# Hyena filter beside the first wave: tap loads up to two quarters ahead, and the Abs tied to the shifted input

## The chip, the cores and the metric

The kernel runs on one core of one Trainium2 chip. The metric is the time of one execution in device microseconds; the kernel before has a median of 2582.66 us in three runs (2580.7 to 2584.5).

## What is computed

One layer of a hybrid backbone: a half-step SwiGLU on the latent tokens `x` and the context tokens `ctx` (256 each, width 2048), token mixing by grouped-query attention and a Hyena long convolution side by side, an output projection, and a second half-step SwiGLU on `x`. Each part is normed and modulated with shift, scale and gate from `w_ada`. Cut to what matters here, with the Hyena filter:

```python
def half_ffn(s, m, slot, g, w_up, w_down):
    h = modulate(rms_norm(s, g), chunk(m, 3 * slot), chunk(m, 3 * slot + 1))
    return s + 0.5 * chunk(m, 3 * slot + 2) * swiglu(h, w_up, w_down)

def hyena_filters(L, w1, b1, w2, b2, w3, b3, w4, freq, decay):
    ...                                    # positional features z, t in 0..1
    h = jnp.sin(fr * (z @ w1 + b1))
    h = jnp.sin(fr * (h @ w2 + b2))
    h = jnp.sin(fr * (h @ w3 + b3))
    h = (h @ w4).reshape(L, 2, HYENA_WIDTH)            # forward and backward half
    h = h * jnp.exp(-t[:, :, None] * jnp.abs(decay)[None])
    ...
    return kk / jnp.sum(jnp.abs(kk), axis=0, keepdims=True)

def reference(x, c, ctx, c_ctx, w_ada, ...):
    mod = silu(c) @ w_ada + b_ada          # 9 chunks of 2048: shift, scale, gate of three parts
    x = half_ffn(x, mod, 0, ...); ctx = half_ffn(ctx, mod_c, 0, ...)
    ...                                    # attention with rotary, Hyena with hyena_filters, output projection
    return half_ffn(x, mod, 2, ...)
```

The filter depends on no token: it is computed from weights alone, `HYENA_WIDTH` = 1024 channels times two halves, and its spectrum is needed only in the token mixing, far behind the first SwiGLU.

## The kernel before

Products are made in fp32 by splitting each operand into a rounded part and a remainder (`hi`, `lo`) and multiplying three times, so each weight tile costs a cast on ScalarE (`whi`) and a subtraction on VectorE (`wlo`).

**The first wave** is the beginning of the first SwiGLU. Nothing of `x` can be multiplied before its shift and scale are known, so the wave runs over the 16 chunks `d` of 128 model columns, and makes three output tiles (`WAVE` = 3) at once, as chunk after chunk of the modulated input comes up. One iteration `d` of the loop at L990 has in its source:

- `row_on(d + 1)`: 32 narrow matmuls (L197) of the conditioning vectors with two row loads `wrow` of 1 MB each, for the modulation of chunk d + 1; then `row_load` of the next row (L184, on SP's queue, four buffers);
- the tile of output 0 (`f1.tile`, L254 to L256), one step of the filter (`next(steps)`), then `col_on(d + 1)`: ScalarE copies the row (L204), TensorE turns it (L206), VectorE finishes shift and scale (L209 to L212), and `wave_h(d + 1)` makes the shifted input: L919 on VectorE, the pair L921 on ScalarE (`f1.shifted` is the second one), L923 on VectorE;
- the tile of output 1, a step; the tile of output 2, a step.

In every fourth iteration three weight tiles of 512 KB are loaded on POOL's queue (L1005, shown at L231), behind a gate, a tiny POOL copy (L1003) of the shift of chunk d, in iterations 1, 5 and 9; the casts and remainders of the tiles in use (L243, L247) are made in iterations 3, 7 and 11.

**The filter** (`filter_spectrum`) is a generator that is stepped between the tiles. After three sine layers (L692 to L714, up to iteration 3) come four quarters `q` of 256 channels, in three iterations each. In source order the Abs of quarter q lies at the beginning of iteration 3q + 4. A quarter does: Abs of the decay row on ScalarE, in place (L725); two Exps (L729) into new tiles; the split of the last layer's weights (L731, L732); the last layer's matmuls (L736, L737), sums and differences (L743, L744), absolute values and their sum (L748 to L754), the transform (L765), and the store of the spectrum to DRAM (`spec`, L773, on POOL's queue). `load_taps(q)` loads the decay rows and the last layer's weights of a quarter: two DMAs each (L684, L687), 128 KB apiece, on POOL's queue, into two tiles of the common pool `U` of 58 tiles of 2 KB a partition. Before, the taps of quarter q + 1 are loaded at the beginning of quarter q (L722), the slot at the end of iteration 3q + 3.

**The order of work.** Dependences, semaphores and buffers are set by a scheduler that orders the instructions of each engine when the program is built. An engine's queue is then worked off strictly in that order. The scheduler may put an instruction ahead of its place in the source when it takes its inputs to be ready. `then(a, do, ...)` (L274) gives it an edge: what `do` issues may not be placed ahead of `a` on the same engine. In the wave nearly all matmuls are chained in this way (`mm = then(mm, ...)`); the filter's steps are not.

## Time and profile before

| | |
|---|---|
| median of three runs | 2582.66 us (2580.7 to 2584.5) |
| the profiled execution | 2580.55 us |
| its span, first to last instruction | 2578.8 us |
| mean granted TensorE clock | 0.997 |
| TensorE busy | 2557.4 us (99%) |
| VectorE / ScalarE / POOL busy | 2164.0 / 1213.6 / 364.0 us |
| HBM read | 558.73 MB |

The profile tells of one execution. Times are microseconds from the first instruction. PE is TensorE's matmuls, PEld its weight loads, DVE VectorE, ACT ScalarE, POOL GpSimd, SP SyncE; a "q" behind the name is the engine's sequencer. `pb<-ident,sg` is what an instruction writes and reads, by the program's tile names. A row of the order of time gives start, duration, engine, line, operation, tiles, shapes, count of merged instructions, and in brackets the idle time of the engine ahead of it and what ended that. A row of the waits gives the waiting instruction, what it waited for, the sum, the count and the longest one. The time of a DMA is that from its issue to its landing. The wave takes about the first 155 us.

### The profile page before, as it was taken

The page shows a single profiled execution, that of the slowest core. Times are in us where ns is not written, and L with a number is a line of the kernel's source. Part 1 is how long each engine was busy: PE and PEld are TensorE (multiplying, and loading weights), DVE is VectorE, ACT ScalarE, POOL GpSimd, SP SyncE. Part 2 cuts the span into 40 slices and gives each one's busy share as a digit, 9 for nine tenths or more (in the row PEclk, how much of TensorE's full clock was granted, in tenths as well). Part 3 has the DMA queues.
Part 4 walks back from the last instruction along what each step waited for, and adds up shares of the span by engine and source line. Part 5 has one row for each costly group of instructions (what it writes and reads, how often), then busy time and mean ns, then how long its engine had stood idle before and what let it go on. Part 6 is the DMA issues. An engine that isn't in the chain of part 4 may idle for free.

```text
span 2578.8 us, 38723 instructions
## 1 busy us (share of the span) xinstructions
PE 2557.4 (99%) x14333; PEld 2199.4 (85%) x14333; DVE 2164.0 (84%) x3498; ACT 1213.6 (47%) x1702; POOL 364.0 (14%) x587
## 2 busy tenths in 40 slices
PE   8999999999999999999999999999999999999999
PEld 5678999999999999888888988888878888888887
DVE  6776888888888886777989796789789899999998
ACT  5353444444444443111211455457466666665554
POOL 1122222222222223320011000000000001012010
PEclk9999999999999999999999999999999999999999
DMA  9988889898888889996798555435757778789784
GB/s 364 355 288 221 233 247 259 240 259 245 244 240 253 250 256 305 395 377 203 258 331 290 185 164 188 131 117 162 233 168 235 247 240 264 238 266 309 236 285 159
DMA packets 209388, 640.77 MB, mean 248 GB/s; under 512 B 24716, under 2 KB 27757, under 8 KB 204845
## 3 DMA queue, kind: packets, MB, share of 16 engines
q1 hardware_dynamic: 134396, 482.37, 55.4%
q0 software_dynamic: 74608, 155.78, 23.3%
q8 instruction: 112, 1.84, 0.3%
q14 instruction: 80, 0.65, 0.1%
q10 hardware_dynamic: 192, 0.13, 0.0%
HBM read 558.73 MB, written 48.53 MB: 235 GB/s over the span
## 4 chain that ended last, share of the span: by engine, by line
PE 96%; DMA 2%; DVE 1%; ACT 0%; issue 0%; POOL 0%; SPq 0%; DVEq 0%; ACTq 0%; POOLq 0%
PE pb L254 10%; PE pb L255 9%; PE pb L256 9%; PE pa L254 9%; PE pa L255 9%; PE pa L256 9%; PE pa L1393 6%; PE pa L1394 6%; PE pa L1395 6%; PE pb L1393 4%; PE pb L1394 4%; PE pb L1395 4%; PE pa L262 3%; PE pa L264 2%; PE pa L1109 1%; PE pa L1110 1%
## 5 line engine op out<-in xcount | busy, mean ns | idle before, releaser
L243 ACT CAST whi<-raw 128x1024 fp32r<-128x1024 f32 x235 | 247.1, 1052 | 499.7 <-PE pb L255 187.8
L247 DVE TENSOR_TENSOR wlo<-raw,whi 128x1024 fp32r<-128x1024 f32 x235 | 286.8, 1221 | 133.7 <-ACT whi L243 131.1
L254 PE MATMUL pa<-u,whi 128*128 128x256 f32 (+1 forms) x912 | 307.4, 338 | 2.1 <-ACT u L906 2.1
L255 PE MATMUL pa<-u,whi 128*128 128x256 f32 (+1 forms) x912 | 305.3, 335 | 0.4 <-DVE u L911 0.4
L256 PE MATMUL pa<-u,wlo 128*128 128x256 f32 (+1 forms) x912 | 305.1, 335 | 0.0
L254 PE MATMUL pb<-u,whi 128*128 128x256 f32 (+1 forms) x904 | 300.2, 332 | 0.0
L255 PE MATMUL pb<-u,whi 128*128 128x256 f32 (+1 forms) x904 | 298.5, 330 | 0.0
L256 PE MATMUL pb<-u,wlo 128*128 128x256 f32 (+1 forms) x904 | 298.4, 330 | 0.0
L466 ACT CAST bhi<-raw 128x768 fp32r<-128x768 f32 x111 | 92.5, 833 | 265.7 <-PE pb L255 132.5
L158 DVE CUSTOM_DVE_ANT_0 adas<-adaw,crow,cond 128x1024 bf16<-128x1024 f32 x160 | 204.9, 1281 | 13.6 <-DMA adaw<-in_w_adaT_dram 11.8
L158 DVE CUSTOM_DVE_ANT_0 adas<-adaw,crow,mod 128x1024 bf16<-128x1024 f32 x160 | 204.9, 1281 | 13.2 <-DMA adaw<-in_w_adaT_dram 11.2
L254 PEld LDWEIGHTS pa<-u,whi 128*128 128x128 f32 x912 | 173.3, 190 | 24.7 <-issue 4.9
L255 PEld LDWEIGHTS pa<-u,whi 128*128 128x128 f32 x912 | 173.6, 190 | 17.5 <-DVE u L911 1.5
L256 PEld LDWEIGHTS pa<-u,wlo 128*128 128x128 f32 x912 | 173.8, 191 | 17.1
L254 PEld LDWEIGHTS pb<-u,whi 128*128 128x128 f32 x904 | 171.8, 190 | 17.4 <-issue 2.0
L469 DVE TENSOR_TENSOR blo<-raw,bhi 128x768 fp32r<-128x768 f32 x111 | 106.2, 957 | 94.6 <-ACT bhi L466 94.6
L255 PEld LDWEIGHTS pb<-u,whi 128*128 128x128 f32 x904 | 171.9, 190 | 15.8 <-issue 0.4
L256 PEld LDWEIGHTS pb<-u,wlo 128*128 128x128 f32 x904 | 171.8, 190 | 15.6
L1395 PE MATMUL pa<-whi,u 128*128 128x512 f32 x451 | 175.7, 390 | 0.0
L1393 PE MATMUL pa<-whi,u 128*128 128x512 f32 x450 | 175.7, 391 | 0.0
L1394 PE MATMUL pa<-wlo,u 128*128 128x512 f32 x450 | 175.6, 390 | 0.0
L277 ACT CAST whi<-raw 128x1024 fp32r<-128x1024 f32 x122 | 126.9, 1052 | 98.2 <-DVE raw L277 62.9
(477 smaller groups left out, 6687.8 us busy)
## 6 DMA issues: line engine op xcount, KB each, us to landing
adaw<-in_w_adaT_dram SPq DMA_DIRECT2D x224, 512.0 KB, 5.9
raw<-in_w_up1q_dram SPq DMA_DIRECT2D x124, 512.0 KB, 5.3
raw<-in_w_up2p_dram SPq DMA_DIRECT2D x107, 512.0 KB, 4.7
raw<-in_w_dn_dram SPq DMA_DIRECT2D x94, 512.0 KB, 5.9
u<-act POOLq DMA_DIRECT2D x172, 256.0 KB, 9.6
wrow<-in_w_ada_dram SPq DMA_DIRECT2D x32, 1024.0 KB, 9.6
raw<-in_w_dn2p_dram SPq DMA_DIRECT2D x59, 512.0 KB, 5.2
vraw<-in_w_up2p_dram SPq DMA_DIRECT2D x53, 512.0 KB, 4.8
```

Of the source, the lines that this page charges most:

```text
L158: V.tensor_tensor_reduce(out=sc, in0=t, in1=crow[i][:, b * (D // 2) : (b + 1) * (D // 2)], scale=1.0, scalar=mcol if b else bada[:, c * KT ...
L243: last_hi[0] = S.copy(hi, raw)
L247: last_lo[0] = V.tensor_sub(lo, raw, hi.bitcast(F32))
L254: PE.matmul(ps, w[0], xx[0], start=start, stop=False)
L255: PE.matmul(ps, w[0], xx[1], start=False, stop=False)
L256: return PE.matmul(ps, w[1], xx[0], start=False, stop=stop)
L277: return do(*args, **kw)
L466: return raw, hi, lo, S.copy(hi, raw[:, :, 0:3])
L469: return V.tensor_sub(lo, raw[:, :, 0:3], hi.bitcast(F32))
L1393: PE.matmul(ps[t], hi, w[0], start=start, stop=False)
L1394: PE.matmul(ps[t], hi, w[1], start=False, stop=False)
L1395: last = PE.matmul(ps[t], lo, w[0], start=False, stop=stop)
```

## The change

Taps are held in a list that is now read from its front. Quarter 0's are loaded in the second sine layer as before; quarter 1's right behind the load of the DFT matrix (`mats`) in the third layer; quarter 2's and 3's in the third step of quarters 0 and 1, behind the sums and differences. The Abs is issued with an edge to `f1.shifted`, the latest shifted input at that point of the source.

```diff
                 mats = U((P, 2, 2, P))
                 nc.gpsimd.dma_start(mats, a["fdft"])
+                taps.append(load_taps(1))
...
         for q in range(4):
-            now = taps.pop()
-            if q < 3:
-                taps.append(load_taps(q + 1))
+            now = taps.pop(0)
             dec, w4 = now
             yield
-            S.activation(dec, dec, AF.Abs)
+            then(f1.shifted, S.activation, dec, dec, AF.Abs)
...
                 V.tensor_sub(pm_[:, 1, :], kt[:, 0, :], kt[:, 1, :])
                 pm.append(pm_)
+            if q < 2:
+                taps.append(load_taps(q + 2))
             yield
```

## The prediction

> **What bounds the kernel now.** I read the page first, then who waited for whom on TensorE, then the order of time around the one long wait, then short stretches.

> ```profile
> span 2578.8 us, 38723 instructions
> ...
> PE 2557.4 (99%) x14333; PEld 2199.4 (85%) x14333; DVE 2164.0 (84%) x3498; ACT 1213.6 (47%) x1702; POOL 364.0 (14%) x587
> ```

> TensorE sets the end. It is idle for 2578.8 - 2557.4 = 21.4 us in all, so a change that leaves the matmuls alone can win no more than that, plus what is lost at a lower clock. TensorE's waits over the whole span:

> ```profile
> PE pb L206 <- ACT sg L204: 4.3, 1, 4.3
> PE pb L197 <- DMA wrow<-in_w_ada_dram: 3.4, 3, 1.9
> ...
> PE pa L1108 <- DVE small L291: 1.2, 1, 1.2
> ```

> The largest is one single wait, and it lies in the first wave, the stage that the diff touches. The order of time there:

> ```profile
> 97.12 1.59 POOL L231 DMA_DIRECT2D raw<-in_w_up_dram  x3 [0.25 <-issue]
> ...
> 98.70 1.07 POOL L684 DMA_DIRECT2D u<-in_flt_decay_dram  x2
> ...
> 110.01 0.40 PE L256 MATMUL pa<-u,wlo 128*128 128x512 f32 x1
> 113.72 0.63 ACT L725 ACTIVATE u<-u 128x512 f32<-128x512 f32 x1 [6.68 <-DMA u<-in_flt_decay_dram]
> 114.26 0.35 ACT L204 COPY sg<-pb 128x256 f32<-128x256 f32 x1
> 114.67 0.44 PE L206 MATMUL pb<-ident,sg 128*128 128x128 f32 x2 [4.26 <-ACT sg L204]
> ```

> Read it from the bottom. At L206 TensorE turns the modulation row of chunk 11 and needs ScalarE's copy L204 for it. Ahead of L204, ScalarE's queue holds L725, the Abs of quarter 3's decay row. By the source that Abs belongs to iteration 13; in the queue it stands in iteration 10, and its data was issued only at 98.70, behind three weight loads. It holds ScalarE until 113.72, and TensorE from 110.41 to 114.67. The wait also costs clock:

> ```profile
> 110.41:114.67 4.26, 0.00 (x1) 0.01 (x1) 0.00 (x0) 0.89 (x2) 0.00 (x0) 1.00 1.01 347
> 115.21:118.62 3.41, 3.41 (x9) 1.94 (x7) 1.80 (x6) 0.91 (x2) 0.00 (x0) 0.50 1.01 422
> ```

> (Length, busy time and count of PE, PEld, DVE, ACT and POOL, granted TensorE clock, DMA share, GB/s.) For 3.41 us after the wait the clock is 0.50, a loss of 3.41 x 0.5 = 1.70 us. A second way to that number: iteration 7 does the same work for quarter 1 without the wait.

> ```profile
> 86.33 0.38 PE L206 MATMUL pb<-ident,sg 128*128 128x128 f32 x2
> ```
> ```profile
> 91.11 1.93 PE L197 MATMUL pb<-wrow,csp 128*32 128x256 f32 x32
> ```
> ```profile
> 121.02 1.93 PE L197 MATMUL pb<-wrow,csp 128*32 128x256 f32 x32
> ```

> From L206 to the next row's L197 it takes 91.11 - 86.33 = 4.78 us there and 121.02 - 114.67 = 6.35 us here: 1.57 us more.

> **The change part by part.** *The tie.* The Abs of a quarter may no longer stand ahead of the latest shifted input, the pair of L921 in the iteration before its own. It moves on ScalarE from behind L731 of the quarter before to behind that L921. ScalarE in iteration 7 now:

> ```profile
> 80.50 0.91 ACT L921 ACTIVATE u<-sq,mod 128x256 fp32r<-128x256 f32 x2 [2.46 <-DVE sq L919]
> 81.31 1.32 ACT L729 ACTIVATE u<-u,u 128x512 f32<-128x512 f32 x2
> 82.54 0.60 ACT L731 CAST u<-u 128x512 fp32r<-128x512 f32 x1
> 83.05 0.63 ACT L725 ACTIVATE u<-u 128x512 f32<-128x512 f32 x1
> 84.98 0.37 ACT L204 COPY sg<-pb 128x256 f32<-128x256 f32 x1 [1.31 <-PE pb L197]
> ```

> The block is L921, the two Exps, the cast, and the Abs of the next quarter. After the change its own Abs (0.63 us) enters ahead of the Exps and the next one's leaves the end, so the block keeps its length, and behind it ScalarE has 1.31 us of idle time ahead of L204. Iteration 10 is alike. Behind the tied Abs are queued the Exps, the cast, L204 and, through it, TensorE: nothing is late if the decay row has landed. In iteration 13 no Abs leaves, so the block grows by 0.63 us; the cover is the 1.31 us of the like place, price 0 (0.63 if it were gone). In iteration 4 the copy stands ahead of the Exps:

> ```profile
> 61.01 0.37 ACT L204 COPY sg<-pb 128x256 f32<-128x256 f32 x1 [1.09 <-PE pb L197]
> ```

> If the Abs falls into the 1.09 us ahead of it, it costs nothing; if it comes behind, the Exps and the cast of quarter 0 are up to 0.63 us later. Between 0 and 0.63 I take 0.1, as the idle time is longer than the Abs. The tie is no wait for another engine: both ends of it are ScalarE's.

> *The loads.* There are sixteen DMAs of 128 KB as before, four a quarter. Quarter 1's stay behind the load of the DFT matrix, one slot earlier; quarter 2's go from iteration 6 of the source to 4, quarter 3's from 9 to 7. What POOL's queue holds there decides what that means:

> ```profile
> 65.82 1.07 POOL L684 DMA_DIRECT2D u<-in_flt_decay_dram  x2
> ...
> 83.81 1.15 POOL L773 DMA_DIRECT2D spec<-u  x2 [15.72 <-DVE u L770]
> 96.57 0.29 POOL L1003 COPY mod<-mod 128x1 f32<-128x1 f32 x1 [11.62 <-DVE mod L212]
> ```

> Quarter 2's loads run at 65.82 already, which is iteration 4. The queues suggest that tiles of the common pool are handed out in source order: the Exps, which write new tiles, stand right behind the L921 of their iteration, while the Abs, which writes in place, runs three iterations ahead. So these loads can hardly go earlier, and I take no move. Quarter 3's come ahead of the gate copy of iteration 9 (96.57), behind the store of quarter 0: issue from 85.0 instead of 98.70, about 2.3 us of POOL in a gap of 11.62 us. Landing of these loads:

> ```profile
> DMA to landing us min/median/max: 11.4/14.8/16.8
> ```

> By 87.3 + 16.8 = 104 us they are there. Thus the loads do a second time for quarter 3 what the tie does alone.

> Their price: 512 KB enter the DMA queues 14 us sooner. The rate there, and in a later stage that a rival needs:

> ```profile
> 80.00:90.00 10.00, 10.00 (x66) 6.65 (x65) 7.32 (x19) 6.45 (x11) 1.15 (x2) 1.00 1.01 366
> 160.00:180.00 20.00, 20.00 (x90) 16.57 (x89) 13.74 (x23) 7.42 (x13) 7.18 (x12) 1.00 1.06 332
> ```

> At 366 GB/s that is 1.4 us for whatever lies behind them. Nearest are the loads of modulation row 10, and its use on TensorE:

> ```profile
> L184 SPq DMA_DIRECT2D wrow<-in_w_ada_dram x2: 328/328/328, 84.1 to 85.0; - x2
> ...
> DMA to landing us min/median/max: 8.0/8.7/9.4
> ```
> ```profile
> 99.56 1.93 PE L197 MATMUL pb<-wrow,csp 128*32 128x256 f32 x32
> ```

> Landed by 85.0 + 9.4 = 94.4 and wanted at 99.56: 5.2 us of room against 1.4. Price 0; with the room gone, 1.4. What is late next, once the wait is gone, is row 12: TensorE would want it at 110.41 + 4.78 = 115.2.

> ```profile
> L184 SPq DMA_DIRECT2D wrow<-in_w_ada_dram x2: 327/328/328, 100.7 to 101.6; - x2
> ...
> DMA to landing us min/median/max: 10.0/11.5/13.0
> ```

> It landed by 101.6 + 13.0 = 114.6, just in time, and will land sooner, since quarter 3's 512 KB no longer share its stretch.

> [...]

> *Sum.* Wait -4.26; clock -1.57 to -1.70, I take -1.64; Abs of iteration 4 +0.1; loads 0: -5.8 us. After the wave TensorE waits for 1.2 us at most at a time (L1108), so an earlier wave is an earlier end. The profiled execution took 2580.55 us, 1.75 more than its span; the median of the runs, 2582.66, lies 2.1 above it. 2580.55 - 5.8 = 2574.75 for a profiled execution, 2576.8 for the median.

> [...]

> **The rivals.** *Handed back in part.* Quarter 2's loads go ahead of the weight loads of iteration 5 after all, into the stretch where TensorE already waits for a row:

> ```profile
> 59.87 1.07 PE L197 MATMUL pb<-wrow,csp 128*32 128x256 f32 x16 [1.86 <-DMA wrow<-in_w_ada_dram]
> ```

> 512 KB there lengthen that wait by up to 1.4 us, and a wait of 3.3 us may cost clock like the other, up to 1.7: 2.7 us of gain are left, 2580.0. For it speaks that the DMAs are full there; against it the order of tiles above.

> *No change.* The stage after the wave is bound by its DMAs (share 1.06 in 160 to 180): its weights come no sooner, and the 5.8 us come back as waits, 2582.7. Against it: TensorE is busy for 20.00 of 20 us in it, so that the weights are ahead of their use.

> *Slower.* POOL's queue is in order. If quarter 3's loads get buffers whose last reader is the store of quarter 1, the gate copy and the weight loads of iteration 9 wait behind them, and ScalarE's casts of these weights wait with L204 of row 13 behind them:

> ```profile
> L773 POOL DMA_DIRECT2D spec<-u x2: 564/578/593, 107.7 to 108.3; - x2
> ...
> DMA to landing us min/median/max: 10.2/10.9/11.6
> ```
> ```profile
> DMA to landing us min/median/max: 6.6/7.7/12.1
> ```
> ```profile
> 128.53 1.04 ACT L243 CAST whi<-raw 128x1024 fp32r<-128x1024 f32 x1 [0.27 <-PE pb L255]
> 131.56 0.37 ACT L204 COPY sg<-pb 128x256 f32<-128x256 f32 x1 [1.99 <-PE pb L197]
> ```

> The store lands at 108.3 + 11.6 = 119.9; loads 2.3 us, weights issued until 123.4, the last landed 12.1 us later (second fence, the three of 97.12), at 135.5. The third cast would then start at 135.5 instead of 128.5 - 5.8 = 122.7, and L204 at 136.6 instead of 125.8: some 10 us of TensorE, and 1.7 of clock, against the 5.8: 2588.6. It decides if fewer than 2 of the pool's 58 tiles are free in iteration 7. Counted from the source there live 8 of x, 18 of shifted input, 5 fixed ones, 10 of two quarters and 4 loaded ahead, 45. So it is unlikely, but any late buffer on POOL works the same way from about 10 us on.

> **How the numbers follow.** Forecast 0.60, its own range 2574.5 to 2578.5; in part 0.18; no change 0.10; slower 0.12. 0.2%, about what a measurement of this kernel can tell from no change, is 5.2 us, so faster means below 2577.5 and slower above 2587.8. Of the forecast's 0.60, 0.52 lie below that; of the last rival's 0.12, 0.08 lie above; the rest is same. The range leaves out the last rival and the ends: 2573.8 to 2583.5.

> **What would show it.** Right: no wait of L206 for L204; no half clock after the start; each L725 behind an L921 and without a wait for the decay row; quarter 3's L684 near 85 us; L197 of row 12 at 115.2. Wrong: a longer wait of L197 for wrow near 60 or 95; L684 waiting on POOL with the weights of iteration 9 behind it; new waits of TensorE after 150 us.

## The result and the profile after

The changed kernel takes 2574.36 us (median of 8 runs, 2573.53 to 2575.39), the kernel before beside it 2581.15 us (8 runs, 2576.57 to 2586.51). The ratio is 0.9974 with a 95% interval of 0.9963 to 0.9984: 6.8 us faster. The forecast was 2576.8 us, 5.8 us faster; the measured median lies 0.14 us below the forecast's own range (2574.5 to 2578.5) and inside the whole range (2573.8 to 2583.5).

The profiled execution took 2573.66 us with a span of 2571.9 us, 6.9 less than before, and a mean granted clock of 0.998. Its head and its longest waits of TensorE:

```profile
span 2571.9 us, 38718 instructions
...
PE 2555.1 (99%) x14333; PEld 2198.3 (85%) x14333; DVE 2164.1 (84%) x3498; ACT 1213.6 (47%) x1702; POOL 365.1 (14%) x587
```
```profile
PE pb L197 <- DMA wrow<-in_w_ada_dram: 3.1, 3, 1.5
PE pa L254 <- ACT u L907: 2.1, 1, 2.1
```

The wait of L206 for L204, the longest of before, is not in the list any more, and no other has come in its place. TensorE's idle time fell from 21.4 us to 2571.9 - 2555.1 = 16.8 us, and its busy time by 2.3 us with the same number of matmuls. The half clock behind the wait is part of that; how much, this pair does not tell, since the second profile of the changed kernel has 2557.3 us again, with half a clock from 17.30 to 30.96 us at its start. ScalarE at the place of the old wait (lines of the changed kernel lie one off here: L922 is the shifted input, L277 is the Abs, recorded at the line of the helper `then`, L728 the Exps):

```profile
103.99 0.91 ACT L922 ACTIVATE u<-sq,mod 128x256 fp32r<-128x256 f32 x2 [2.46 <-DVE sq L920]
104.81 0.62 ACT L277 ACTIVATE u<-u 128x512 f32<-128x512 f32 x1
105.46 1.34 ACT L728 ACTIVATE u<-u,u 128x512 f32<-128x512 f32 x2
...
108.48 0.37 ACT L204 COPY sg<-pb 128x256 f32<-128x256 f32 x1 [1.18 <-PE pb L197]
```

The Abs that runs here now is that of its own quarter, without idle time ahead of it. The copy L204 waits only for the row's matmuls, as it should. TensorE goes from chunk 11's turning to row 12 without a stop and at full clock:

```profile
109.60 0.39 PE L256 MATMUL pa<-u,wlo 128*128 128x512 f32 x1
109.83 0.38 PE L206 MATMUL pb<-ident,sg 128*128 128x128 f32 x2
...
114.60 1.72 PE L197 MATMUL pb<-wrow,csp 128*32 128x256 f32 x28
```
```profile
109.83:114.60 4.77, 4.77 (x19) 2.95 (x17) 4.03 (x11) 0.91 (x2) 0.00 (x0) 1.00 1.01 418
```

From L206 to row 12 it takes 4.77 us at clock 1.00, 6.35 us before. Counted from L256, the last matmul ahead of L206, so with the wait, it is 114.60 - 109.60 = 5.00 us, and 121.02 - 110.01 = 11.01 before: 6.01 us less. POOL's queue, with quarter 3's loads ahead of the gate copy:

```profile
65.89 1.08 POOL L684 DMA_DIRECT2D u<-in_flt_decay_dram  x2
...
84.54 1.08 POOL L684 DMA_DIRECT2D u<-in_flt_decay_dram  x2
...
96.17 0.30 POOL L1004 COPY mod<-mod 128x1 f32<-128x1 f32 x1 [9.36 <-DVE mod L212]
```

Quarter 2's loads have not moved (65.89, before 65.82). Quarter 3's have, from 98.70 to 84.54.

### The profile page after: what moved, and what is told of

Same layout as the page of the kernel before. It is cut to its first block, busy times and chain, and to the rows that moved or that the text cites. A ratio compares the mean times of both kernels' runs of the same rounds, so it can differ in the third digit from the quotient of the medians.

```text
span 2571.9 us, 38718 instructions
## 1 busy us (share of the span) xinstructions
PE 2555.1 (99%) x14333; PEld 2198.3 (85%) x14333; DVE 2164.1 (84%) x3498; ACT 1213.6 (47%) x1702; POOL 365.1 (14%) x587
## 4 chain that ended last, share of the span: by engine, by line
PE 97%; DMA 1%; DVE 1%; ACT 0%; issue 0%; SPq 0%; ACTq 0%; DVEq 0%
PE pb L254 10%; PE pb L255 10%; PE pb L256 10%; PE pa L254 9%; PE pa L255 9%; PE pa L256 9%; PE pa L1394 6%; PE pa L1395 6%; PE pa L1396 6%; PE pb L1394 4%; PE pb L1396 4%; PE pb L1395 4%; PE pa L262 3%; PE pa L264 2%; PE pa L1110 1%; PE pa L1111 1%
## 5 line engine op out<-in xcount | busy, mean ns | idle before, releaser
L243 ACT CAST whi<-raw 128x1024 fp32r<-128x1024 f32 x235 | 247.2, 1052 | 500.4 <-PE pb L255 192.3
L255 PE MATMUL pa<-u,whi 128*128 128x256 f32 (+1 forms) x912 | 304.8, 334 | 0.9 <-DVE u L912 0.9
L256 PE MATMUL pa<-u,wlo 128*128 128x256 f32 (+1 forms) x912 | 304.5, 334 | 0.0
L255 PE MATMUL pb<-u,whi 128*128 128x256 f32 (+1 forms) x904 | 298.4, 330 | 0.0
L256 PE MATMUL pb<-u,wlo 128*128 128x256 f32 (+1 forms) x904 | 298.3, 330 | 0.0
L255 PEld LDWEIGHTS pa<-u,whi 128*128 128x128 f32 x912 | 173.5, 190 | 17.7 <-DVE u L912 1.7
L256 PEld LDWEIGHTS pa<-u,wlo 128*128 128x128 f32 x912 | 173.5, 190 | 17.2
L255 PEld LDWEIGHTS pb<-u,whi 128*128 128x128 f32 x904 | 171.9, 190 | 15.7 <-issue 0.4
L256 PEld LDWEIGHTS pb<-u,wlo 128*128 128x128 f32 x904 | 171.8, 190 | 15.6
L277 ACT CAST whi<-raw 128x1024 fp32r<-128x1024 f32 x122 | 126.9, 1052 | 98.4 <-DVE raw L277 63.0
```

The source lines that it names most:

```text
L243: last_hi[0] = S.copy(hi, raw)
L255: PE.matmul(ps, w[0], xx[1], start=False, stop=False)
L256: return PE.matmul(ps, w[1], xx[0], start=False, stop=stop)
L277: return do(*args, **kw)
```

## The experiments

**The tie alone, and the loads alone.** Two edits of the kernel before, each one half of the change.

```diff
-            S.activation(dec, dec, AF.Abs)
+            then(f1.shifted, S.activation, dec, dec, AF.Abs)
```

> The kernel before with the tie alone; the loads stay where they were (quarter 3's issued behind the three weight loads of iteration 9, near 98 us). Theory 'place in the queue' (the wait is there because the Abs stands in ScalarE's queue three iterations early): the wait of L206 for L204 goes with its half clock, the Abs of quarter 3 runs near 129 us without a wait, time 2574 to 2576, equal to the changed kernel within 1.5 us. Rival 'late data' (the taps have to come sooner): the decay row still lands near 113 us and row 12 near 114.6, so a wait of 1 us or more stays near 110 to 116 us, 2577 to 2581.

Measured: 2575.76 us (2574.13 to 2577.01) against 2581.32 of the kernel before, ratio 0.9975 (0.9965 to 0.9985), span 2574.0. POOL's queue is that of before, so quarter 3's loads stand behind the weights as ever:

```profile
97.44 1.58 POOL L231 DMA_DIRECT2D raw<-in_w_up_dram  x3 [0.19 <-issue]
99.02 1.08 POOL L684 DMA_DIRECT2D u<-in_flt_decay_dram  x2
```
```profile
109.27 0.37 ACT L204 COPY sg<-pb 128x256 f32<-128x256 f32 x1 [1.18 <-PE pb L197]
```
```profile
110.63 0.38 PE L206 MATMUL pb<-ident,sg 128*128 128x128 f32 x2
...
115.40 1.93 PE L197 MATMUL pb<-wrow,csp 128*32 128x256 f32 x32
```

L204 has the same 1.18 us of idle time ahead of it as in the changed kernel, TensorE the same 4.77 us to row 12. In the wave the tie alone yields the whole result; where the 1.4 us between its median and that of the changed kernel come from is told further down. That the data comes late no longer matters, as nobody stands in the queue for it. The rival 'late data' expected a wait of 1 us or more to stay here, and there is none.

The loads alone are the other lines of the diff, with the plain Abs:

```diff
+                taps.append(load_taps(1))
...
-            now = taps.pop()
-            if q < 3:
-                taps.append(load_taps(q + 1))
+            now = taps.pop(0)
...
+            if q < 2:
+                taps.append(load_taps(q + 2))
```

> The changed kernel without the tie: loads up to two quarters ahead, the Abs free to be placed early. On ScalarE's queue the Abs of quarter 2 then stands in iteration 5 behind L749 (70 us in the changed kernel), that of quarter 3 in iteration 8 (94 us). Theory 'place in the queue': quarter 2's decay row lands at 82 to 84 us, so ScalarE stands for some 12 us from 70, the shifted input of chunk 6 comes near 86 instead of 72.7, TensorE wants it at 77: a wait of about 9 us, 1.7 us of half clock, and perhaps a second short wait in iteration 8: 2583 to 2590, slower than before. Rival 'late data': earlier loads suffice, the wait is gone, 2574 to 2577.

Measured: 2586.18 us (2584.48 to 2588.34), ratio 1.0016 (1.0008 to 1.0025), span 2586.5: slower than before. ScalarE's and TensorE's order of time, and the clock:

```profile
69.85 1.16 ACT L749 ACTIVATE u<-u 128x512 f32<-128x512 f32 x2
82.55 0.63 ACT L724 ACTIVATE u<-u 128x512 f32<-128x512 f32 x1 [11.54 <-DMA u<-in_flt_decay_dram]
...
84.13 0.36 ACT L759 COPY mt<-pb 1x256 f32<-1x256 f32 x1
...
106.22 0.63 ACT L724 ACTIVATE u<-u 128x512 f32<-128x512 f32 x1 [0.72 <-DMA u<-in_flt_decay_dram]
```
```profile
84.54 3.64 PE L197 MATMUL pb<-wrow,csp 128*32 128x256 f32 x32 [8.42 <-ACT mt L759]
```
```profile
78.43:88.67 10.24, 4.13 (x33) 1.88 (x34) 4.32 (x7) 2.31 (x6) 0.00 (x0) 0.50 0.36 100
```

With the loads earlier in the source, the scheduler puts the Abs earlier as well: quarter 2's stands right behind L749 of iteration 5, and holds ScalarE for 11.54 us and TensorE for 8.42 us. So asking for the data earlier does not help when the Abs moves up with its load. Quarter 3's Abs, at 106.22, waited only 0.72 us, and TensorE did not wait for it.

The profile is that of the slowest of the eleven runs, 14.6 us longer in span than the one of the changed kernel. Of these, 8.42 us are the wait and about 2.1 the clock behind it (84.54 to 88.67 at 0.50), as expected in place and size. At like matmuls (the same one of the program in both profiles), 0.8 us were there before the wait, 1.4 us come with one more stretch at half clock, 1505.20 to 1508.61 us (last section), and 2.0 us between 1510 and 1880 us, at full clock; the cause of the last ones is open.

**Weights behind the taps.** Is the wait gone too when only quarter 3's data comes early and the Abs keeps its bad place? And what does a late buffer on POOL cost (the prediction's slower rival)? In the kernel before, the gate copy of iteration 9 gets an order edge behind the last load of quarter 3; nothing else is touched.

```diff
+                if d == 9:
+                    order.enter_context(tc.issue_after(last_tap[0].ins))
+                gate = G.tensor_copy(warm, mod[0][0][:, d : d + 1])
```

> The kernel before with one edge on POOL alone: the gate and the three weight loads of iteration 9 stand behind quarter 3's taps. ScalarE's queue has its old order, the Abs of quarter 3 three iterations early. The taps then go out near 85 us and land by 100, ahead of that Abs (107 us): both theories expect the wait of L204 gone. What it tells apart is the rival of the prediction by which late weights on POOL's queue make the kernel slower: the weights now also stand behind the store of quarter 1, near 109 us instead of 97, and land at 115 to 122 us, while ScalarE wants to cast them at 118, 120.3 and 122. If they are in time: 2574 to 2576. If not: up to 3 us more, 2577 to 2579.

Measured: 2577.26 us (2575.79 to 2578.8), ratio 0.9982 (0.9973 to 0.9991), span 2575.4. POOL and ScalarE:

```profile
85.23 1.07 POOL L686 DMA_DIRECT2D u<-in_flt_decay_dram  x2
...
108.00 1.15 POOL L775 DMA_DIRECT2D spec<-u  x2 [20.50 <-DVE u L772]
...
109.26 1.58 POOL L231 DMA_DIRECT2D raw<-in_w_up_dram  x3
```
```profile
107.24 0.63 ACT L727 ACTIVATE u<-u 128x512 f32<-128x512 f32 x1
109.23 0.37 ACT L204 COPY sg<-pb 128x256 f32<-128x256 f32 x1 [1.36 <-PE pb L197]
...
126.81 1.05 ACT L243 CAST whi<-raw 128x1024 fp32r<-128x1024 f32 x1 [2.18 <-DMA raw<-in_w_up_dram]
```

The Abs at 107.24 is still three iterations ahead of its quarter, and waits for nothing: with early data the bad place is harmless here. So the old wait needed both, the early place and the late data. As expected, the scheduler put the store of quarter 1 ahead of the gate copy, so that the weights are issued at 109.26 instead of 97.12, and the third cast starts at 126.81. TensorE had one wait from it:

```profile
124.68 1.93 PE L197 MATMUL pb<-wrow,csp 128*32 128x256 f32 x32 [0.85 <-ACT mt L760]
```

The slower rival's way from late weights over ScalarE's casts to TensorE is real, but 12 us of delay of these weights cost TensorE a wait of 0.85 us, and 1.2 us at like matmuls by the end of the wave (against the second profile of the changed kernel). The time lies where it was expected for weights that come too late, 2577 to 2579, but not by these alone: of the 2.9 us between this kernel and the changed one, 1.5 us come in the profiles with a stretch at half clock near 1495 us (last section).

**The changed kernel again, and one wait more.** The changed kernel unchanged, for the spread between its profiles:

> The changed kernel once more, on the chip of the others: 2574.4 within 1.5 us by every theory, with no wait of L206 and a wait of about 1.5 us for the row near 59 us.

Measured: 2574.37 us (2573.99 to 2575.16), ratio 0.997 (0.9958 to 0.9981), span 2572.5. There is no wait of L206. L256 ahead of it starts at 109.60, 110.29 and 109.71 in the three profiles of the changed kernel, so what lies before differs by up to 0.7 us from one execution to the other.

The longest wait left in the wave behind that for its first tile (2.08 us, at 25.46) is row 5's, at 59.48, for a row load that is under way while quarter 1's loads are (POOL issues them from 42.03 to 51.98), at a DMA share of 1.02 from 45 to 60 us. A gate copy, which waits for the modulation of chunk 4, now holds the DFT matrix and quarter 1's loads back:

```diff
-                nc.gpsimd.dma_start(mats, a["fdft"])
-                taps.append(load_taps(1))
+                gate = G.tensor_copy(warm, mod[0][0][:, 4:5])
+                with tc.issue_after(gate.ins):
+                    nc.gpsimd.dma_start(mats, a["fdft"])
+                    taps.append(load_taps(1))
```

> The changed kernel with one step more: the load of the DFT matrix and quarter 1's taps wait on POOL for a gate copy of the shift of chunk 4 (about 55 us), instead of going out at 41 to 52 us. Theory 'the tie frees the loads': with the Abs of quarter 1 tied to 80 us, its taps need not stand ahead of the modulation row of chunk 5, so 0.77 MB leave the queue ahead of that row; its wait near 58 us (1.3 to 1.9 us in the traces so far) falls to 0 to 0.3, and the kernel is 1.0 to 1.7 us faster than the changed one: 2572.7 to 2573.5. Rival 'full DMA': the DMAs are full from 10 to 110 us, so the row that is late is only another one (chunk 6 or 7), or the matrix is late at its use near 73 us: 2574 to 2577.

Measured: 2574.42 us (2573.01 to 2576.72), ratio 0.998 (0.9971 to 0.9989), and for the changed kernel of the same batch:

> The changed kernel beside the gated one, for comparison on the same chip: 2574.4 within 1.5 us, with the row's wait near 58 us.

2575.15 us (2573.9 to 2576.48), ratio 0.9981 (0.9972 to 0.9989). The two differ by 0.7 us, less than either one's own spread. Row 5 in the changed kernel, then the same stretch with the gate:

```profile
59.48 1.07 PE L197 MATMUL pb<-wrow,csp 128*32 128x256 f32 x16 [1.54 <-DMA wrow<-in_w_ada_dram]
60.48 0.73 PE L254 MATMUL pa<-u,whi 128*128 128x512 f32 x2
```
```profile
57.55 1.93 PE L197 MATMUL pb<-wrow,csp 128*32 128x256 f32 x32
60.29 0.73 PE L254 MATMUL pa<-u,whi 128*128 128x512 f32 x2 [0.81 <-ACT u L924]
```

The row's wait is gone, and TensorE runs into the next late thing, chunk 4's shifted input (L924), which on ScalarE stands behind the filter's last sine (L704), and that one had waited 0.50 us for VectorE. Of the wait, 0.2 us is left as a gain at 60.29 against this profile. The expected 1.0 to 1.7 us did not come; the time lies in the range of the rival 'full DMA', though what was late next was neither a row nor the matrix. So there is no version here that can be said to beat the changed kernel.

**The kernel before, profiled again.** Its times spread over 10 us in the first comparison, those of the changed kernel over 2. Does the wait itself vary, or what the clock makes of it? Two more profiles of the kernel before, unchanged:

> The kernel before once more, for a second trace. Its times spread over some 8 us and those of the changed kernel over 2. Theory 'late data': the wait of L206 for the Abs differs from run to run by microseconds, since it ends with a landing in full DMA queues; 2 to 8 us in this trace, with or without half clock. Rival 'clock phase': the wait is 4.2 us again and only the half clock differs, by 1.7 us at most.

> The same for a third trace of the kernel before: the wait of L206 differs from 4.26 us by 1 us or more in at least one of the two traces by the theory 'late data', and in neither by the rival 'clock phase'.

Measured: 2580.5 us with a span of 2578.7, and 2581.87 us with 2580.1. The wait and the clock behind it, first for the second profile, then for the third:

```profile
109.59 0.40 PE L256 MATMUL pa<-u,wlo 128*128 128x512 f32 x1
114.18 0.69 PE L206 MATMUL pb<-ident,sg 128*128 128x128 f32 x2 [4.19 <-ACT sg L204]
...
121.18 1.93 PE L197 MATMUL pb<-wrow,csp 128*32 128x256 f32 x32
...
112.22:119.05 6.83, 4.87 (x11) 3.04 (x11) 2.24 (x7) 1.80 (x4) 0.00 (x0) 0.50 0.96 397
```
```profile
111.36 0.40 PE L256 MATMUL pa<-u,wlo 128*128 128x512 f32 x1
115.46 0.56 PE L206 MATMUL pb<-ident,sg 128*128 128x128 f32 x2 [3.70 <-ACT sg L204]
...
121.84 1.93 PE L197 MATMUL pb<-wrow,csp 128*32 128x256 f32 x32
...
115.63:119.04 3.41, 3.41 (x10) 2.27 (x9) 1.80 (x6) 0.91 (x2) 0.00 (x0) 0.50 1.01 423
61.02:64.43 3.41, 3.41 (x11) 2.61 (x10) 1.53 (x5) 3.38 (x6) 0.11 (x1) 0.50 1.01 354
```

The wait is 4.26, 4.19 and 3.70 us in three profiles. Neither new one differs from the first by 1 us, so the theory 'late data' as it was put is refuted, and the rival holds for the wait. The half clock behind it lasts 3.41, 6.83 and 3.41 us, and the third profile has one more such stretch, 61.02 to 64.43, behind the 1.79 us wait for row 5. From L256 to row 12 the three take 11.01, 11.59 and 10.48 us, against 5.00 in each of the three profiles of the changed kernel: the wait and the clock behind it cost 6.0, 6.6 and 5.5 us.

That is not all of the 10 us. The mean granted clock of the 25 runs of the kernel before that stand beside the tie alone goes with the longest times: the five at 0.994 took 2583.9 to 2585.9 us, the ten at 0.997 or more 2578.65 to 2582.56 us, the ten between 2577.98 to 2584.28 us. This suggests that the clock has a larger share in the spread than the three profiles show, but it is not shown which stretches bring it.

## Why the prediction was right

**The wait, -4.26 us.** Right in place, cause and size. L206 no longer waits, and the tie alone shows that taking the Abs out of its place on ScalarE is enough. The stretch from L256 to row 12, wait and clock together, became 6.01 us shorter, against 4.26 + 1.64 = 5.90 in the sum.

**The clock, -1.64 us.** Right against the profile that it was worked out from: 6.35 us from L206 to row 12 became 4.77, which is 1.58. As a price of such a wait in general it is too narrow: the second profile of before paid 6.83 us at half clock. The upper end of the prediction's own range, 2578.5, stands for runs of before whose wait brings no half clock, with 4.2 us to win; that was the author's estimate, and no run shows such a wait. Behind waits of 4.26, 4.19 and 3.70 us the three profiles have 3.41, 6.83 and 3.41 us at 0.50. In the first the half clock sets in at 115.21, behind the wait (110.41 to 114.67); in the second at 112.22, inside the wait (109.99 to 114.18), and it lasts until 119.05.

**The Abs of iteration 4, +0.1 us, and of iteration 13, 0.** It fell into idle time:

```profile
59.48 0.61 ACT L277 ACTIVATE u<-u 128x512 f32<-128x512 f32 x1
60.67 0.37 ACT L204 COPY sg<-pb 128x256 f32<-128x256 f32 x1 [0.58 <-PE pb L197]
```
```profile
132.38 0.37 ACT L204 COPY sg<-pb 128x256 f32<-128x256 f32 x1 [0.99 <-PE pb L197]
```

0.58 us of idle time remain ahead of L204 in iteration 4, and 0.99 in iteration 13: both cost nothing.

**The loads, 0.** Right for the sum. At like matmuls the tie alone and the second profile of the changed kernel stay within 0.2 us of each other from 62 to 1490 us; then the tie alone loses 1.3 us near 1494 us, to 3.42 us at half clock shown below. By one profile of each, that is most of the 1.4 us between the medians, and it lies outside the wave. But one reason given was only half right: "the loads do a second time for quarter 3 what the tie does alone". Without the tie they nearly did so for quarter 3, whose Abs still waited for 0.72 us. But the scheduler, which the prediction itself names, moves an unbound Abs up after its load, and quarter 2's cost TensorE 8.4 us. The prediction has no term for that, and it needed none only because the tie stands beside the loads. Early data alone does help where the Abs stays put, as the weights behind the taps showed.

**Row 12 as the next late thing.** It was expected at 115.2 and started at 114.60 in the first profile, at 115.29 in the second. The prediction had its load landing sooner, since quarter 3's loads no longer share its stretch. This is the row load's time from issue to landing in the changed kernel (first fence) and with the tie alone (second):

```profile
L184 SPq DMA_DIRECT2D wrow<-in_w_ada_dram x2: 328/330/331, 100.3 to 101.2; - x2
...
DMA to landing us min/median/max: 9.8/11.2/12.6
```
```profile
L184 SPq DMA_DIRECT2D wrow<-in_w_ada_dram x2: 328/330/331, 101.1 to 101.9; - x2
...
DMA to landing us min/median/max: 10.9/12.2/13.5
```

With the tie alone the last half lands at 101.9 + 13.5 = 115.4, as L197 starts (115.40). In the changed kernel it lands at 101.2 + 12.6 = 113.8, 0.8 us ahead of 114.60. That is what the earlier loads bring: no time, but some room.

**The rivals.** Handed back in part: refuted, the loads of quarter 2 stayed at 65.89 and row 5's wait did not grow (1.54, before 1.86). No change: refuted, the stage after the wave kept the whole lead:

```profile
160.00:180.00 20.00, 20.00 (x90) 16.57 (x89) 13.88 (x22) 4.73 (x7) 4.68 (x7) 1.00 1.07 344
```

TensorE is busy for all of it, as before. Slower: quarter 3's loads did not wait for a buffer (84.54). Its price, 10 us of TensorE, rested on loads that wait for the landing of a store; where the weights were only queued behind the store's issue, TensorE waited for 0.85 us.

**The time, 2576.8 against 2574.36.** Of the 2.4 us, 1.5 are the base: the kernel before had a median of 2582.66 in the runs that the prediction started from, and 2581.15 beside the changed kernel. That the base came out high was the chance of three runs. The rest is 1.0 us of gain beyond 5.8. In the first pair of profiles 0.4 us of the lead is there before the wait (L256 at 110.01 and 109.60), a place where the changed kernel differs from itself by up to 0.7 us; against the second profile of the changed kernel the lead is 5.7 to 6.0 us at like matmuls after the wave. In the batch of the gated kernel, on another chip than the tie alone, the gain was 2579.57 - 2575.15 = 4.4 us; beside the tie alone it was 2581.32 - 2574.37 = 6.95. So 5.8 lies between the gains that were measured, and the further 1.0 us has no cause that these runs show.

## What to carry to other kernels

When an engine waits for a small copy on another, look at what stands ahead of that copy in the other's queue, and in which iteration of the source it belongs: here an instruction of three iterations later blocked it. Tie such an instruction behind the last urgent one rather than load its data earlier: here the loads moved up let the scheduler move their reader up as well, and that alone made the kernel slower (2586.18 us against 2581.32). The waits of 3.70 to 4.26 us cost their own length and 3.41 or 6.83 us at half clock, 5.5 to 6.6 us in all, so sum the clock with the wait, and take the spread from more than one profile.

## What the runs showed of the hardware

```profile
1491.38 0.61 PE L306 MATMUL pb<-ones,sg 128*128 128x2 f32 x4
...
1494.45 0.63 PE L1108 MATMUL pa<-whi,u 128*128 128x512 f32 x1
```
```profile
1490.79:1494.20 3.41, 3.41 (x23) 2.81 (x22) 3.41 (x7) 2.24 (x6) 0.00 (x0) 1.00 0.15 60
1494.20:1497.62 3.42, 3.42 (x10) 2.68 (x9) 2.47 (x6) 0.46 (x2) 0.00 (x0) 0.50 0.71 208
```

TensorE is busy for all 3.41 us of the first stretch, and the next has half the clock; a 512-column matmul takes 0.63 us there instead of 0.39. The loads alone have the same: 3.41 us of busy TensorE from 1501.79 to 1505.20 at clock 1.00, then 3.41 us at 0.50, and the weights behind the taps have such a stretch near 1495 us. In the first profiles of before and of the changed kernel the group starts at 1497.02 and 1490.58; the grid, counted on from the last change of the clock, has an edge inside it, at 1497.61 and 1491.00, and the clock stays full. In the gated kernel the group runs from 1490.59 to 1492.54, and the 512-column matmuls behind it take 0.39 to 0.40 us from 1492.85 on.

Not every such group costs clock, though. Some 29 us earlier stand another 16 matmuls of two columns, in 1.70 us between matmuls of 256 columns. In the first profile of before they lie wholly within 1466.89 to 1470.30, one step of the grid counted on in the same way, and the step behind it has the full clock:

```profile
1468.02 0.51 PE L306 MATMUL pa<-ones,sg 128*128 128x2 f32 x4
...
1470.30:1473.71 3.41, 3.41 (x31) 3.41 (x30) 1.89 (x6) 1.47 (x3) 0.00 (x0) 1.00 0.39 102
```

So the half clock followed only the group of 1.95 us, and not in every profile; why is not shown. It was not tied to idle time alone: it came behind 3.41 us without any (the tie alone), and in the second profile of before behind 3.41 us with 1.18 us of matmuls at full clock in them (108.81 to 109.99, half clock from 112.22). Nor does the length of a wait tell: behind row 5's wait of 1.86 us in the first profile of before (until 59.87) the clock stayed at 1.00, from 29.88 to 115.21, behind that of 1.79 us in the third it was 0.50 from 61.02 to 64.43. For timing it means that a difference of 1 to 2 us between two of these kernels may be one such stretch alone: it came to 1.3 us with the tie alone, 1.4 us with the loads alone and 1.5 us with the weights behind the taps.
